# RMSNorm on one core: every second group's sums of squares go through PSUM, squared four rows at a time on ScalarE and summed on VectorE

## The chip, the cores and the metric

The kernel runs on one core of a Trainium2 chip. The metric is the device time of one execution in microseconds (us). For the kernel before it is 163.68 us, the median of 10 runs that lie between 163.41 and 164.09.

## The reference

```python
def reference(x, gamma):              # x: 16 x 1024 x 512 f32, gamma: 512
    eps = 1e-5
    rms = np.sqrt(np.mean(x ** 2, axis=-1, keepdims=True) + eps)
    return (x / rms * gamma).astype(np.float32)
```

There are 16,384 rows of 512 values. Each row is divided by the root of the mean of its squares and multiplied by gamma. The kernel reads 33.55 MB and writes as much.

## The kernel before

The rows are cut into four blocks of 4,096 rows (8.39 MB each). In a block each of the 128 partitions holds 32 rows of 512 values. SBUF has three buffers of that size, `slot0` to `slot2`; blocks 0, 1 and 2 each get one, and block 3 is loaded into `slot0` once block 0 has been stored from there.

**Transfers.** All large transfers are issued by SyncE (SP), in one queue, in the order of the program: block 0 in two halves of 16 rows (called load 0a and load 0b here), block 1, block 2; then store 0 (whole), store 1a (rows 0 to 15), load 3a, load 3b, store 1b, store 2 (whole), store 3a, store 3b. SP waits at each one until what it needs is there: a store for the multiplies of its rows, load 3a and load 3b for the landing of store 0 (they overwrite its buffer). What stands behind a waiting transfer is not issued until the wait is over. Half a block is 4.19 MB.

**Computation.** `compute(slot, r0, r1)` walks over groups of `G = 8` rows. There are 16 groups in all, numbered 0 to 15 here: 0 to 3 are block 0, 4 to 7 block 1, and so on; store 0 needs groups 0 to 3, store 1a groups 4 and 5, store 1b groups 6 and 7, store 2 groups 8 to 11, store 3a groups 12 and 13, store 3b groups 14 and 15. For each group:

- ScalarE squares each row by itself (line 70) and accumulates the sum of the squares into one column of `ss`; on the engine this is an ACTIVATE and a short ACTIVATION_READ_ACCUMULATOR. The squares themselves go to `sq_scratch` and are not read.
- ScalarE takes the root of `ss / 512 + eps` into `rms` (line 76). The first root is preceded by a table load.
- VectorE takes the reciprocal into `rstd` (line 77) and multiplies each row, in place, by its `rstd` and by gamma (line 79, one SCALAR_TENSOR_TENSOR for each row).

Each engine works through its own queue in order. Before the loop gamma is spread over the 128 partitions by a matmul with a column of ones (line 56) and copied from PSUM to SBUF by VectorE (line 58). The order on ScalarE and VectorE before is that of the program: eight squares and a root for each group on ScalarE, a reciprocal and eight multiplies for each group on VectorE.

Of the kernel before, what the change touches and what calls it, by code (L numbers as in the profile page):

```python
# [1 line left out]

# [4 lines left out]


@with_exitstack
def kernel(  # L10
    ctx: ExitStack,
    tc: tile.TileContext,
    x: bass.AP,
    gamma: bass.AP,
    out: bass.AP,
):
    nc = tc.nc
    P = nc.NUM_PARTITIONS
    eps = 1e-5
    fp32 = mybir.dt.float32  # L20
    AF = mybir.ActivationFunctionType
    OP = mybir.AluOpType

    xf = x.flatten_outer_dims()
    of = out.flatten_outer_dims()
    N, D = xf.shape
    R = 32
    G = 8
    assert N == 4 * P * R

    xv = xf.rearrange("(t p r) d -> t p r d", p=P, r=R)
    ov = of.rearrange("(t p r) d -> t p r d", p=P, r=R)

    const = ctx.enter_context(tc.tile_pool(name="const", bufs=1))
    stats = ctx.enter_context(tc.tile_pool(name="stats", bufs=4))
    psum = ctx.enter_context(tc.tile_pool(name="psum", bufs=1, space=bass.MemoryType.PSUM))

    slots = [const.tile([P, R, D], fp32, name=f"slot{i}") for i in range(3)]

    def load(t, slot, r0, r1):  # L40
        nc.sync.dma_start(out=slots[slot][:, r0:r1], in_=xv[t][:, r0:r1])

    def store(t, slot, r0, r1):
        nc.sync.dma_start(out=ov[t][:, r0:r1], in_=slots[slot][:, r0:r1])

    load(0, 0, 0, 16)
    load(0, 0, 16, 32)
    load(1, 1, 0, 32)
    load(2, 2, 0, 32)

    gamma_row = const.tile([1, D], fp32)
    nc.scalar.dma_start(out=gamma_row, in_=gamma.unsqueeze(0))
    ones_col = const.tile([1, P], fp32)
    nc.vector.memset(ones_col, 1.0)  # L54
    gamma_psum = psum.tile([P, D], fp32)
    nc.tensor.matmul(gamma_psum, ones_col, gamma_row, start=True, stop=True)  # L56
    gamma_b = const.tile([P, D], fp32)
    nc.vector.tensor_copy(out=gamma_b, in_=gamma_psum)  # L58

    eps_t = const.tile([P, 1], fp32)  # L60
    nc.vector.memset(eps_t, eps)  # L61
    sq_scratch = const.tile([P, D], fp32)

    def compute(slot, r0, r1):
        for g in range(r0, r1, G):
            ss = stats.tile([P, G], fp32, name="ss")
            rms = stats.tile([P, G], fp32, name="rms")
            rstd = stats.tile([P, G], fp32, name="rstd")
            for r in range(G):
                nc.scalar.activation(  # L70
                    out=sq_scratch,
                    in_=slots[slot][:, g + r, :],
                    func=AF.Square,
                    accum_out=ss[:, r : r + 1],
                )
            nc.scalar.activation(out=rms, in_=ss, func=AF.Sqrt, bias=eps_t, scale=1.0 / D)  # L76
            nc.vector.reciprocal(out=rstd, in_=rms)  # L77
            for r in range(G):
                nc.vector.scalar_tensor_tensor(  # L79
                    out=slots[slot][:, g + r, :],  # L80
                    in0=slots[slot][:, g + r, :],
                    scalar=rstd[:, r : r + 1],
                    in1=gamma_b,
                    op0=OP.mult,
                    op1=OP.mult,
                )

    compute(0, 0, 32)
    store(0, 0, 0, 32)
    compute(1, 0, 16)  # L90
    store(1, 1, 0, 16)
    load(3, 0, 0, 16)
    load(3, 0, 16, 32)
    compute(1, 16, 32)
    store(1, 1, 16, 32)
    compute(2, 0, 32)
    store(2, 2, 0, 32)
    compute(0, 0, 16)
    store(3, 0, 0, 16)
    compute(0, 16, 32)  # L100
    store(3, 0, 16, 32)


# [1 line left out]
_INS = ['x', 'gamma']  # L105
_OUTS = [((16, 1024, 512), 'float32')]


# [23 lines left out]
```

## Time and profile before

| | before |
|---|---|
| median of 10 runs | 163.68 us |
| the profiled execution | 163.41 us |
| its span | 161.6 us |
| VectorE idle before the first reciprocal, until a root came | 15.27 us, ended at 20.41 us |
| HBM read and written | 33.56 MB and 33.55 MB, 415 GB/s over the span |

The span is the part of the execution that the trace covers, from its first to its last record; 1.8 us of the execution lie outside it. All points in time count from the start of the span. In the page, L70 is line 70, ACT is ScalarE and DVE is VectorE, and a row of the list of groups gives operation, output and input, shapes, number, then busy time in all and the mean of one in ns, then the idle time of the engine just before these instructions. The DMA row of the picture in slices has a digit for each fortieth of the span, the busy share of the 16 DMA engines in tenths.

### The profile page before, as it was taken

Reading aid. Unit: us, or ns where it says so; the run is one execution under the profiler, and the core shown is the slowest. Engines: PE = TensorE matmul, PEld = TensorE weight load, DVE = VectorE, ACT = ScalarE, POOL = GpSimd, SP = SyncE. Lnnn points to the kernel's source line nnn. Section 1 sums busy time; section 2 is a strip of 40 time slices with the busy share of each in tenths; the row PEclk is TensorE's granted clock in tenths of the full one; section 3 lists DMA queues with packets and bytes.
Section 4 is the critical chain, followed back from the end, with each engine's and each line's share of the span. In section 5 each row is a group of like instructions: output and inputs, shape, how many; then the busy total and the mean of one; then the engine's idle time right before and its main releaser. Section 6 shows DMA issues by size and latency. Waiting matters only on the chain.

```text
span 161.6 us, 509 instructions
## 1 busy us (share of the span) xinstructions
PE 2.0 (1%) x2; PEld 0.5 (0%) x2; DVE 90.3 (56%) x147; ACT 98.5 (61%) x274; POOL 0.2 (0%) x4
## 2 busy tenths in 40 slices
PE   4000000000000000000000000000000000000000
PEld 1000000000000000000000000000000000000000
DVE  0100098988909898898898892019889890000000
ACT  3008999996599999999999700699999400000000
POOL 0000000000000000000000000000000000000000
DMA  7999999998998999699699999999999799799990
GB/s 260 389 414 495 389 438 470 519 391 389 519 405 373 505 276 487 292 503 503 292 481 414 397 487 414 397 487 414 397 511 503 341 454 503 308 462 414 422 462 41
DMA packets 1733, 67.14 MB, mean 415 GB/s; under 512 B 193, under 2 KB 193, under 8 KB 194
## 3 DMA queue, kind: packets, MB, share of 16 engines
q1 hardware_dynamic: 1728, 67.11, 97.2%
q14 instruction: 3, 0.02, 0.0%
q10 hardware_dynamic: 2, 0.00, 0.0%
HBM read 33.56 MB, written 33.55 MB: 415 GB/s over the span
## 4 chain that ended last, share of the span: by engine, by line
DMA 43%; ACT 20%; DVE 17%; issue 2%; DVEq 0%
DMA out_dram<-slot 24%; DMA slot<-in_x_dram 19%; ACT sq_scratch L70 18%; DVE slot L79 16%; ACT rms L76 2%; ACT L76 1%; DVE rstd L77 1%; DVEq L127 0%
## 5 line engine op out<-in xcount | busy, mean ns | idle before, releaser
L70 ACT ACTIVATE sq_scratch<-slot 128x512 f32<-128x512 f32 x128 | 80.5, 629 | 27.0 <-DMA slot<-in_x_dram 23.5
L79 DVE SCALAR_TENSOR_TENSOR slot<-slot,rstd,gamma_b 128x512 f32<-128x512 f32 x128 | 86.2, 747 | 0.6
L77 DVE RECIPROCAL rstd<-rms 128x8 f32<-128x8 f32 x16 | 3.2, 203 | 37.8 <-ACT rms L76 37.8
L70 ACT ACTIVATION_READ_ACCUMULATOR sq_scratch<-slot 128x1 f32 x128 | 23.9, 187 | 0.0
L76 ACT ACTIVATE rms<-ss,eps_t 128x8 f32<-128x8 f32 x16 | 4.8, 301 | 0.5
L58 DVE COPY gamma_b<-gamma_psum 128x512 f32<-128x512 f32 x1 | 0.7, 692 | 3.5 <-PE gamma_psum L56 3.5
L56 PE MATMUL gamma_psum<-gamma_row,ones_col 1*128 1x512 f32 x2 | 2.0, 1122 | 2.4 <-DMA gamma_row<-in_gamma_dram 2.4
L70 ACT ACT_TABLE_LOAD x1 | 1.3, 1283 | 1.3 <-PEq L116 1.3
L76 ACT ACT_TABLE_LOAD x1 | 1.3, 1283 | 0.0
L54 DVE MEMSET ones_col<- 1x128 f32 x1 | 0.2, 165 | 0.8 <-PEq L116 0.8
L56 PEld LDWEIGHTS gamma_psum<-gamma_row,ones_col 1*128 1x128 f32 x2 | 0.5, 306 | 2.3 <-issue 2.3
L116 POOL MEMSET const-bfloat16-1.0<- 128x1 bf16 x1 | 0.1, 101 | 0.0
L116 POOL MEMSET const-uint8-127<- 128x1 uint8 x1 | 0.1, 101 | 0.0
L116 POOL MEMSET const-float32-0.0<- 128x1 f32 x1 | 0.1, 98 | 0.2 <-issue 0.2
L116 POOL MEMSET const-float32-1.0<- 128x1 f32 x1 | 0.1, 98 | 0.0
L61 DVE MEMSET eps_t<- 128x1 f32 x1 | 0.1, 59 | 0.0
## 6 DMA issues: line engine op xcount, KB each, us to landing
slot<-in_x_dram SPq DMA_DIRECT2D x4, 4096.0 KB, 19.4
out_dram<-slot SPq DMA_DIRECT2D x4, 4096.0 KB, 31.2
slot<-in_x_dram SPq DMA_DIRECT2D x2, 51.0
out_dram<-slot SPq DMA_DIRECT2D x2, 40.7
gamma_row<-in_gamma_dram ACTq DMA_DIRECT2D x1, 2.0 KB
```

The source lines that it names most:

```text
L54: nc.vector.memset(ones_col, 1.0)
L56: nc.tensor.matmul(gamma_psum, ones_col, gamma_row, start=True, stop=True)
L58: nc.vector.tensor_copy(out=gamma_b, in_=gamma_psum)
L61: nc.vector.memset(eps_t, eps)
L70: nc.scalar.activation(out=sq_scratch, in_=slots[slot][:, g + r, :], func=AF.Square, accum_out=ss[:, r : r + 1],)
L76: nc.scalar.activation(out=rms, in_=ss, func=AF.Sqrt, bias=eps_t, scale=1.0 / D)
L77: nc.vector.reciprocal(out=rstd, in_=rms)
L79: nc.vector.scalar_tensor_tensor(out=slots[slot][:, g + r, :], in0=slots[slot][:, g + r, :], scalar=rstd[:, r : r + 1], in1=gamma_b, op0=O ...
L116: nc = _bacc.Bacc("TRN2", target_bir_lowering=False, num_devices=1)
```

## The change

In the groups with an odd number the eight accumulating squares are replaced. ScalarE squares four rows with one instruction (128 partitions x 2,048 values) into a PSUM tile `sq`, and VectorE sums each of the four rows in it with one `tensor_reduce`, into four columns of `ss`. Two such pairs make a group. `sq` takes 8 KB of each partition, and the pool has two of them. The tile in which gamma is spread now comes from the same pool. The even groups stay as they were.

```diff
+    H = 4
-    psum = ctx.enter_context(tc.tile_pool(name="psum", bufs=1, space=bass.MemoryType.PSUM))
+    psum = ctx.enter_context(tc.tile_pool(name="psum", bufs=2, space=bass.MemoryType.PSUM))
...
-    gamma_psum = psum.tile([P, D], fp32)
-    nc.tensor.matmul(gamma_psum, ones_col, gamma_row, start=True, stop=True)
+    gamma_psum = psum.tile([P, H, D], fp32, name="sq")
+    nc.tensor.matmul(gamma_psum[:, 0], ones_col, gamma_row, start=True, stop=True)
     gamma_b = const.tile([P, D], fp32)
-    nc.vector.tensor_copy(out=gamma_b, in_=gamma_psum)
+    nc.vector.tensor_copy(out=gamma_b, in_=gamma_psum[:, 0])
...
-            for r in range(G):
-                nc.scalar.activation(
-                    out=sq_scratch,
-                    in_=slots[slot][:, g + r, :],
-                    func=AF.Square,
-                    accum_out=ss[:, r : r + 1],
-                )
+            if (g // G) % 2:
+                for h in range(0, G, H):
+                    sq = psum.tile([P, H, D], fp32, name="sq")
+                    nc.scalar.activation(out=sq, in_=slots[slot][:, g + h : g + h + H, :], func=AF.Square)
+                    nc.vector.tensor_reduce(
+                        out=ss[:, h : h + H], in_=sq, axis=mybir.AxisListType.X, op=OP.add
+                    )
+            else:
+                for r in range(G):
+                    nc.scalar.activation(
+                        out=sq_scratch,
+                        in_=slots[slot][:, g + r, :],
+                        func=AF.Square,
+                        accum_out=ss[:, r : r + 1],
+                    )
             nc.scalar.activation(out=rms, in_=ss, func=AF.Sqrt, bias=eps_t, scale=1.0 / D)
```

The layer under the kernel orders the instructions of an engine by itself, and with this change it interleaves groups. The two queues of the changed program are, with q4 x1 for one accumulating square of a row of group 4, S5a and S5b for the two four-row squares of group 5, R5a and R5b for their sums, rt4 for the root, rc4 for the reciprocal and m4 for the eight multiplies of group 4:

```
ScalarE
q0 x1, S1a, q0 x1, S1b, q0 x6, table load, rt0, rt1
q2 x1, S3a, q2 x1, S3b, q2 x6, rt2, rt3
q4 x1, S5a, q4 x1, S5b, q4 x1, S7a, q4 x1, S7b, q4 x4, rt4, rt5
q6 x8, rt6
q8 x1, S9a, q8 x7, q10 x1, rt7, rt8
S9b, q10 x1, S11a, q10 x6, rt9, rt10, S11b, rt11
q12 x1, S13a, q12 x1, S13b, q12 x6, rt12, rt13
q14 x1, S15a, q14 x1, S15b, q14 x6, rt14, rt15

VectorE
R1a, R1b, rc0, rc1, m0, m1
R3a, rc2, R3b, m2, rc3, m3
R5a, R5b, rc4, R7a, m4, rc5, rc6, m5, m6
R7b, R9a, rc7, rc8, m7, m8
R9b, R11a, rc9, rc10, m9, m10, R11b, rc11, m11
R13a, R13b, rc12, rc13, m12, m13
R15a, rc14, R15b, m14, rc15, m15
```

The order of the transfers on SP is unchanged.

## The prediction

> **What bounds the kernel now.** First the page's slices and DMA queues, to see whether a resource is full.
>
> ```profile
> PE 2.0 (1%) x2; PEld 0.5 (0%) x2; DVE 90.3 (56%) x147; ACT 98.5 (61%) x274; POOL 0.2 (0%) x4
> DMA  7999999998998999699699999999999799799990
> q1 hardware_dynamic: 1728, 67.11, 97.2%
> ```
>
> SP's queue keeps the 16 DMA engines busy for 97.2% of the span; no compute engine passes 61%. The kernel is bound by its transfers, and computation matters only where it hands over a store after the queue has run empty. So next: how late may each store come? The chain of waits, the timeline of VectorE's last group and the DMA answer for the last store:
>
> ```profile
> 0.72 12.02 DMA slot<-in_x_dram
> ...
> 44.75 38.12 DMA out_dram<-slot
> ```
> ```profile
> 127.33 0.20 DVE L77 RECIPROCAL rstd<-rms 128x8 f32<-128x8 f32 x1 [0.61 <-ACT rms L76]
> 127.57 5.39 DVE L79 SCALAR_TENSOR_TENSOR slot<-slot,rstd,gamma_b 128x512 f32<-128x512 f32 x8
> ```
> ```profile
> out_dram<-slot SPq DMA_DIRECT2D x1, 4096.0 KB, 27.6
> ```
>
> A half block into an empty queue lands 12.02 us after its issue. The last store is issued at 133.0, when the multiplies end, and lands 27.6 us later, at 160.6: over half of that is queueing. The DMA records (packets of the queue, split by their 4-byte markers) show the transfers strictly in turn, 9.68 us for each half block. Counting back 1.0 us from issue to first packet, no DMA engine idles if store 0 is issued by 60.5, store 1a by 79.8, store 1b by 108.9, store 2 by 118.5, store 3a by 137.9 and store 3b by 147.5. Before, they come at 44.8, 60.6, 83.8, 98, 120.5 and 133.0: 14.5 to 25 us early. **That margin of 14.5 us at the last store is what the change may spend.** It can gain next to nothing, since earlier stores would only queue.
>
> **The prices.** The list of groups:
>
> ```profile
> L70 ACT ACTIVATE sq_scratch<-slot 128x512 f32<-128x512 f32 x128 | 80.5, 629 | 27.0 <-DMA slot<-in_x_dram 23.5
> L79 DVE SCALAR_TENSOR_TENSOR slot<-slot,rstd,gamma_b 128x512 f32<-128x512 f32 x128 | 86.2, 747 | 0.6
> L77 DVE RECIPROCAL rstd<-rms 128x8 f32<-128x8 f32 x16 | 3.2, 203 | 37.8 <-ACT rms L76 37.8
> L70 ACT ACTIVATION_READ_ACCUMULATOR sq_scratch<-slot 128x1 f32 x128 | 23.9, 187 | 0.0
> L76 ACT ACTIVATE rms<-ss,eps_t 128x8 f32<-128x8 f32 x16 | 4.8, 301 | 0.5
> L58 DVE COPY gamma_b<-gamma_psum 128x512 f32<-128x512 f32 x1 | 0.7, 692 | 3.5 <-PE gamma_psum L56 3.5
> ```
>
> Instructions overlap, so I use steps, not means. Multiplies: eight take 5.39 = 7 steps + 0.747, a step of 0.665 and a tail of 0.08. Accumulating square with its read: 0.752 (pairs in the chain start that far apart). Root 0.31, table load 1.3, reciprocal up to the next multiply 0.24.
>
> - **Removed from ScalarE:** 64 accumulating squares, 64 x 0.752 = 48.1 us.
> - **Added to ScalarE:** 16 four-row squares, 128x2048. Not in the trace. From below: the squares against the root, (629 - 301) / 504 = 0.65 ns a value, give 0.629 + 1536 x 0.65 ns = 1.63. From above: four separate ones, 2.52. [...]
> - **Added to VectorE:** 16 sums of 128x2048 from PSUM. Not in the trace. From above: four times the nearest row, the copy of 512 from PSUM, less overlap: 4 x 0.692 - 0.08 = 2.69. [...] Multiply against reciprocal, (747 - 203) / 504 = 1.08 ns a value, gives 0.692 + 1.66 - 0.08 = 2.27. I take **2.25**. Sum 36.0; VectorE goes from 90 to 126 us busy.
>
> [...]
>
> **The walk through the queues.** The built order decides how much of the 36 us is hidden.
>
> 1. ScalarE starts at 12.76, when load 0a lands. Ahead of root 0 it now has 8 x 0.752 + 2 x 1.83 + 1.3 + 0.31 = 11.3. The first reciprocal starts at 24.08 (before 20.41); sums R1a and R1b lie in that wait, free.
> 2. From there VectorE has 128 x 0.665 = 85.1, 16 x 0.24 = 3.8 and 14 x 2.25 = 31.5, together 120.4, and is nearly always the later engine.
> 3. One real hole. ScalarE's S7a and S7b stand ahead of root 4 and need PSUM tiles that R5a and R5b free; these stand behind group 3's multiplies, which end at 51.0. R5a ends at 53.2, R5b at 55.4; from 53.2 ScalarE needs 2 x 1.83 + 5 x 0.752 + 0.31 = 7.7 to finish root 4 at 61.0. **VectorE idles 5.6 us.** ScalarE's own waits there (5.0 for a tile) cost nothing further.
> 4. Small holes: R11b, root 11, reciprocal 11 in turn, 0.44; others 0.3. Root 11 holds back all of block 3 on ScalarE (until 113.9), but its transfers landed by 112.3 and groups 12 and 13 are ready before VectorE is.
>
> Sum: 24.1 + 120.4 + 5.6 + 0.8 + 0.1 = **151.0**, the issue of store 3b, 18 us later than before. The same walk gives 51.0 for store 0, 74.7, 90.3, 119.5 and 135.3 for the others: only store 2 (by 1 us) and store 3b (by 3.5) come after the queue may idle, and store 3b alone sets the end. The waits that SP gains on ScalarE for load 3a and 3b are for squares long done.
>
> The end: 151.0 + 11.8 = 162.8, against 160.6. I take 11.8 rather than 12.02, because the first packets of load 0a took 1.5 to 2.1 us where later ones take 1.21. The loss is less than 3.5 because an empty queue lets the lagging DMA engine catch up: the last store's parts landed over 2.0 us before. So 163.41 + 2.2 = **165.6 us**. The profiled execution was among the shortest of the ten; I add nothing for the median (0.27 higher), since the new path never waits for a transfer after 12.76.
>
> Zero lies at an issue by 160.6 - 11.8 = 148.8. From the walk, 0.1 us on a sum moves the end by 1.3, on a four-row square by 0.4.
>
> **The rivals.**
>
> - **The margin holds (not slower), 16%.** Mechanism: VectorE's sum is cheap enough. Place: the 13 sums on its path; point: below 2.08 us each, or other steps 2.2 us shorter in all, the last store is issued by 148.8. For it: the margin is large and my overlap guesses are coarse. [...] Half of this I count as within 0.2%, half as faster.
> - **The sum pays per row, 8%.** If each 512-value row costs like the copy, 2.69: issue 156.8, end 168.6, time 171.4. [...]
> - **VectorE late by the forecast, 76%.** Sums 2.13 to 2.4 and squares 1.63 to 1.95 give 163.9 to 168.4.
>
> That the change doesn't act is out: the built queues hold the 16 squares and 16 sums.
>
> Range 163.4 to 168.8, leaving out the per-row case and about half of the first. A measurement of this kernel tells 0.2% (0.33 us) from no change. Slower 0.83, same 0.08, faster 0.09.
>
> **What would show it.** VectorE near 126 us busy, with the new row of sums at 2.3 us mean (tail included) and four-row squares at 1.9; the first reciprocal at 24.1; a VectorE hole of 5 to 6 us before reciprocal 4, around 55 to 61; last multiplies ending at 151; the last store landing 11.5 to 12 us after its issue instead of 27.6; the DMA share dipping just before 152. A last store that still queues for well over 12 us would mean that the margin held; sums far from 2.3 us would break the sum.

## The result and the profile after

The changed kernel takes 162.63 us, the median of 14 runs (162.28 to 163.32). The kernel before takes 163.59 us, the median of 51 runs with those on the same chips (162.72 to 164.50). The ratio is 0.9942, interval 0.9928 to 0.9955: **faster by 0.6%**, where 165.6 us and slower had been forecast. The profiled execution took 162.42 us, its span is 160.6 us.

These are the lines of the page after: engine totals, DMA picture, the two DMA queues, and the rows of the groups that changed.

```profile
span 160.6 us, 402 instructions
...
PE 2.0 (1%) x2; PEld 0.5 (0%) x2; DVE 123.4 (77%) x163; ACT 79.9 (50%) x162; POOL 0.2 (0%) x4
...
DMA  7999999969969999898999999999996996999993
...
q1 hardware_dynamic: 1728, 67.11, 97.8%
q14 instruction: 2, 0.02, 0.0%
...
L88 DVE SCALAR_TENSOR_TENSOR slot<-slot,rstd,gamma_b 128x512 f32<-128x512 f32 x128 | 85.7, 747 | 0.1
L79 ACT ACTIVATE sq_scratch<-slot 128x512 f32<-128x512 f32 x64 | 40.0, 625 | 13.8 <-DMA slot<-in_x_dram 12.5
L74 DVE TENSOR_REDUCE ss<-sq 128x4 f32<-128x2048 f32 x16 | 36.1, 2277 | 10.5 <-ACT sq L73 10.4
L73 ACT ACTIVATE sq<-slot 128x2048 f32<-128x2048 f32 x16 | 29.7, 1859 | 4.8 <-DVE ss L74 4.8
```

VectorE did take on the forecast load (123.4 us), ScalarE did become lighter (98.5 to 79.9 us), and the transfers stay the full resource (97.8%). The same two queue lines before show what the forecast passed over:

```profile
span 161.6 us, 509 instructions
...
q1 hardware_dynamic: 1728, 67.11, 97.2%
q14 instruction: 3, 0.02, 0.0%
```

Queue 14, of the kind "instruction" in the page, fetches the program's own instructions, 8,192 bytes each time in the DMA records, on the same 16 DMA engines: at each fetch of the two executions one of the engines leaves a gap of 0.30 us between two packets of data. Before there are three such fetches in the span, after there are two. In the DMA records they start at 33.9, 53.3 and 83.0 us before, at 45.9 and 64.2 after.

The stores, from VectorE's timeline after (start, duration, instruction, idle time before it): its hole in the middle, and its end.

```profile
49.90 4.48 DVE L74 TENSOR_REDUCE ss<-sq 128x4 f32<-128x2048 f32 x2
59.77 0.20 DVE L86 RECIPROCAL rstd<-rms 128x8 f32<-128x8 f32 x1 [5.39 <-ACT rms L85]
...
142.17 0.20 DVE L86 RECIPROCAL rstd<-rms 128x8 f32<-128x8 f32 x1
142.40 5.39 DVE L88 SCALAR_TENSOR_TENSOR slot<-slot,rstd,gamma_b 128x512 f32<-128x512 f32 x8
```

The hole before reciprocal 4 is there. The last multiplies end at 147.8, not at 151.0. The view of that last store alone, after:

```profile
L45 SPq DMA_DIRECT2D out_dram<-slot x1: 332/332/332, 147.8 to 147.8; - x1
...
DMA to landing us min/median/max: 11.8/11.8/11.8
```

It lands at 147.8 + 11.8 = 159.6, 1 us ahead of the 160.6 before, although it was issued 14.8 us later.

**Where the microsecond came from.** The DMA records hold a 4-byte marker for each DMA engine at the end of each transfer (192 in each execution, for 12 transfers), so they show how far the 16 engines are apart. The engine that finishes first is nearly the same in the two executions: its store 3a ends at 148.5 before and 148.4 after. The last one differs. Spread between first and last engine, in us, at the end of six of the transfers:

| | load 0b | block 1 | block 2 | store 1a | load 3b | store 3a |
|---|---|---|---|---|---|---|
| before | 0.54 | 0.96 | 1.70 | 1.70 | 2.05 | 2.05 |
| after | 0.36 | 0.36 | 0.94 | 1.08 | 1.19 | 1.19 |

Every transfer here is cut into equal shares for the 16 engines (1,728 packets, 108 for each engine over the whole kernel), so one that has fallen behind stays behind (1.70 us before from block 2 to store 1a, 2.05 from load 3b to store 3a), and the last landing is that of the slowest. The 1.0 us between the two landings is this spread (2.05 - 1.19 = 0.86) and the 0.13 of the fastest engine. The packets of one engine follow each other within a few ns, so they can be strung together engine by engine. An engine that took a fetch started its next packet 0.30 us late, and that packet took longer as well: 2.73, 3.02 and 1.33 us at the three fetches before, where 2.42, 2.42 and 1.21 are usual in this trace. So a fetch put its engine back by 0.6, 0.9 and 0.4 us.

Before, the fetches at 33.9 and 83.0 fell on one DMA engine, which ended 1.53 behind the first. The fetch at 53.3 fell on another, which lost 0.45 more in a stretch near 58 in which all engines were slow, and 0.35 in a single packet at 109. That one is the last, 2.05 behind. So in this one execution the fetch that is missing after the change, the one at 83.0, did not set the end; what its absence is worth has to come from the runs below. In "after" the slowest engine never ran dry: 149.6 + 9.68 = 159.3, its marker of the last store. So a late store that lets lagging engines catch up can't have made the gain here.

### The profile page after: what moved, and what is told of

Read it like the earlier page. It is cut to its first block, busy times and chain, and to the rows that moved or that the text cites. A ratio compares the mean times of both kernels' runs of the same rounds, so it can differ in the third digit from the quotient of the medians.

```text
span 160.6 us, 402 instructions
## 1 busy us (share of the span) xinstructions
PE 2.0 (1%) x2; PEld 0.5 (0%) x2; DVE 123.4 (77%) x163; ACT 79.9 (50%) x162; POOL 0.2 (0%) x4
## 3 DMA queue, kind: packets, MB, share of 16 engines
q1 hardware_dynamic: 1728, 67.11, 97.8%
## 4 chain that ended last, share of the span: by engine, by line
DVE 71%; ACT 12%; DMA 7%; issue 1%; DVEq 0%
DVE slot L88 52%; DVE ss L74 18%; DMA slot<-in_x_dram 7%; ACT sq_scratch L79 6%; ACT sq L73 4%; DVE rstd L86 1%; ACT L85 1%; ACT rms L85 1%; DVEq L136 0%
## 5 line engine op out<-in xcount | busy, mean ns | idle before, releaser
L79 ACT ACTIVATE sq_scratch<-slot 128x512 f32<-128x512 f32 x64 | 40.0, 625 | 13.8 <-DMA slot<-in_x_dram 12.5
L74 DVE TENSOR_REDUCE ss<-sq 128x4 f32<-128x2048 f32 x16 | 36.1, 2277 | 10.5 <-ACT sq L73 10.4
L73 ACT ACTIVATE sq<-slot 128x2048 f32<-128x2048 f32 x16 | 29.7, 1859 | 4.8 <-DVE ss L74 4.8
L79 ACT ACTIVATION_READ_ACCUMULATOR sq_scratch<-slot 128x1 f32 x64 | 11.9, 186 | 0.0
L59 DVE COPY gamma_b<-sq 128x512 f32<-128x512 f32 x1 | 0.7, 692 | 3.2 <-PE sq L57 3.2
L57 PE MATMUL sq<-gamma_row,ones_col 1*128 1x512 f32 x2 | 2.0, 1122 | 2.1 <-DMA gamma_row<-in_gamma_dram 2.1
L57 PEld LDWEIGHTS sq<-gamma_row,ones_col 1*128 1x128 f32 x2 | 0.5, 308 | 2.1 <-issue 2.1
```

The lines of the kernel that those rows point to most:

```text
L57: nc.tensor.matmul(gamma_psum[:, 0], ones_col, gamma_row, start=True, stop=True)
L59: nc.vector.tensor_copy(out=gamma_b, in_=gamma_psum[:, 0])
L73: nc.scalar.activation(out=sq, in_=slots[slot][:, g + h : g + h + H, :], func=AF.Square)
L74: nc.vector.tensor_reduce(out=ss[:, h : h + H], in_=sq, axis=mybir.AxisListType.X, op=OP.add)
L79: nc.scalar.activation(out=sq_scratch, in_=slots[slot][:, g + r, :], func=AF.Square, accum_out=ss[:, r : r + 1],)
```

## The experiments

Theory F says that fewer instructions on ScalarE mean fewer fetches, and that the lag which fetches cause in single DMA engines sets the end. Rivals: D, the late last store empties the queue and lets laggards catch up; T, VectorE's walk still ends the kernel; C, the gain comes from other order or lighter traffic, or the lags are chance. Eleven kernels were run, all in several rounds against the kernel before on the same chips. Fetches and spread are those of each run's profiled execution; the spread is that at the end of store 3a, as above.

| run | median us | ratio to before (interval) | fetches | spread |
|---|---|---|---|---|
| short_sum | 162.58 | 0.9938 (0.9917 to 0.9958) | 2 | 1.33 |
| transfers | 162.15 | 0.9902 (0.9877 to 0.9928) | 0 | 1.07 |
| transfers_fill | 164.99 | 1.0073 (1.0044 to 1.0102) | 4 | 3.56 |
| after_fill | 164.86 | 1.0064 (1.0044 to 1.0084) | 6 | 3.59 |
| act_fill | 163.10 | 0.9979 (0.9964 to 0.9994) | 3 | 1.55 |
| no_sums | 162.59 | 0.9950 (0.9935 to 0.9965) | 2 | 0.96 |
| late | 165.04 | 1.0099 (1.0067 to 1.0131) | 2 | 1.62 |
| before_shift | 163.41 | 0.9995 (0.9976 to 1.0014) | 3 | 2.16 |
| after_fill1 | 163.76 | 1.0015 (1.0000 to 1.0030) | 4 | 2.56 |
| no_sums_fill | 163.23 | 1.0001 (0.9977 to 1.0026) | 3 | 2.01 |
| scratch_psum | 163.39 | 1.0005 (0.9987 to 1.0023) | 3 | 1.50 |

That the spread sets the end holds throughout: the time of the profiled execution less its spread is between 161.2 and 161.6 us in all of them, the kernels before and after included, except in late (163.4), whose queue ran dry. But the spread of one execution has chance in it: late is the changed kernel up to its last group and has 1.62 where the change has 1.19. What an edit costs is therefore read from the medians.

**short_sum**, on the changed kernel:

```diff
-                        out=ss[:, h : h + H], in_=sq, axis=mybir.AxisListType.X, op=OP.add
+                        out=ss[:, h : h + H], in_=sq[:, :, 0:128], axis=mybir.AxisListType.X, op=OP.add
```

> The changed kernel, but each sum reads only the first 128 of the 512 squares of a row, so that sums over a quarter of the values are computed in the odd groups. Same number of instructions on each engine as the change, VectorE some 20 us earlier at the end. Theory F (fewer instructions on ScalarE mean fewer instruction fetches, each of which holds one DMA engine up; the lag of that engine sets the end): still 2 fetches, the time stays at 162.2 to 162.8, although the last store is issued near 127 and queues for over 30 us. Rival D (the late last store finds the queue running dry, which lets lagging DMA engines catch up): with the store early again the gain goes, 163.3 to 163.8. Rival T (VectorE's walk is still what ends the kernel): 161.5 or less.

162.58 us. The last store alone:

```profile
L45 SPq DMA_DIRECT2D out_dram<-slot x1: 332/332/332, 134.9 to 134.9; - x1
...
DMA to landing us min/median/max: 25.2/25.2/25.2
```

It is issued at 135, some 13 us earlier than in the change (less than the 20 expected) and queues again, and the time is that of the change. D and T fall: neither a late last store nor VectorE's end decides in the changed kernel.

**transfers**, on the kernel before:

```diff
-    compute(0, 0, 32)
     store(0, 0, 0, 32)
-    compute(1, 0, 16)
     store(1, 1, 0, 16)
...
```

> Only the transfers: the normalization is left out and the output is the input; the twelve transfers and the preparation of gamma stay, in the same order on SP. The floor of the transfers. Theory F: no instruction fetch in the span, the DMA engines end within 0.7 us of each other, time 161.3 to 162.2, below the change. Rival D: no store comes late, lags add up as before, 163.2 to 163.8. Rival C (lags are chance and contention on memory, whatever the instructions): between, 162.3 to 163.3.

162.15 us, without a fetch in the span. This is the floor of these twelve transfers: the kernel before stands 1.6 us above it in the same rounds (163.75), the change about 0.5. The spread of the profiled execution, one of its longer ones, was somewhat wider than the 0.7 expected; half of it came near 109, in one step and without any fetch.

**transfers_fill** (on transfers) and **after_fill** (on the change), the same edit:

```diff
+    fill = const.tile([P, 1], fp32)
+    for i in range(512):
+        nc.gpsimd.memset(fill, float(i))
     gamma_row = const.tile([1, D], fp32)
```

> The transfers alone as in the run beside it, with 512 memsets of 128x1 on GpSimd, which nothing waits for. Theory F: some four instruction fetches of 8 KB appear in the span, each holds one DMA engine up by 0.4 to 0.9 us, on one engine where it is the same program's queue; the last landing comes 0.7 to 3 us later than in the run without them. Rivals C and D: no change within 0.3 us.

> The changed kernel with 512 memsets of 128x1 on GpSimd, which nothing waits for; VectorE and ScalarE as in the change. Theory F: four more fetches, 163.3 to 165.3. Rivals C and D: 162.3 to 163.0 as the change.

164.99 us against 162.15, and 164.86 against 162.63: 2.2 to 2.8 us for memsets that nobody waits for. The queue lines of transfers_fill:

```profile
q1 hardware_dynamic: 1728, 67.11, 96.3%
q14 instruction: 4, 0.03, 0.0%
```

They share no data with the transfers. The DMA records of transfers_fill show how they act: 15 engines stay within 0.71 us of each other to the end, and one falls behind, 0.82 by load 0b, 1.49 after the fetch at 32.2, 3.09 by the end of block 2, 3.49 after the fetch at 71.8. All four fetches (11.0, 32.2, 52.2, 71.8) struck the same engine, and its share of the last store is what the kernel waits for. Not all of its lag is the fetches themselves: of the 1.60 gained in block 2, the fetch at 52.2 is 0.66, and the rest was lost in the slow stretch that follows, near 58 to 61. Rivals C and D fall for these runs.

**act_fill**, on the change: give ScalarE back enough instructions for a second fetch.

```diff
+    fill = const.tile([P, 1], fp32)
+    for i in range(40):
+        nc.scalar.activation(out=fill, in_=eps_t, func=AF.Square)
+
     def compute(slot, r0, r1):
```

> The changed kernel with 40 squares of 128x1 put ahead of the first square on ScalarE, in the time in which it waits for load 0a; VectorE's queue and the stores as in the change. It gives ScalarE over 200 instructions again, enough to reach a second instruction fetch (before fetched for ScalarE near its 60th and 191st instruction). Theory F: 3 fetches in the span, two of them holding up the same DMA engine; the last landing 0.4 to 0.9 us later than with the change, time 162.9 to 163.6. Rival C (the gain came from the lighter traffic of ScalarE, or from the order of the groups): no change, 162.3 to 162.8.

163.10 us: half of the gain is gone. The page has the third fetch, and in the DMA records it comes at 120.8, when ScalarE has started 184 instructions. ScalarE's two fetches are at 17.0 and 120.8, not at 33.9 and 83.0; both fall on one DMA engine, and it is the last one (1.55). The other half of the gain is not explained by this run.

```profile
q1 hardware_dynamic: 1728, 67.11, 97.5%
q14 instruction: 3, 0.02, 0.0%
```

**no_sums**, on the change: the ScalarE half alone.

```diff
                     nc.scalar.activation(out=sq, in_=slots[slot][:, g + h : g + h + H, :], func=AF.Square)
-                    nc.vector.tensor_reduce(
-                        out=ss[:, h : h + H], in_=sq, axis=mybir.AxisListType.X, op=OP.add
-                    )
+                ss = ones_ss
```

> The ScalarE half of the change alone: four-row squares in the odd groups, but VectorE doesn't sum them; the root of these groups is taken of a constant. The sums of squares of the odd groups are left out. Last store issued some 30 us before the change's. Theory F: 2 fetches, 162.2 to 162.8, as the change. Rival D (a late last store gives the gain): 163.3 or more. If VectorE's later end costs the change anything: up to 0.2 us below it.

162.59 us. The whole gain is in the ScalarE half; the 36 us of sums on VectorE cost nothing that can be measured.

**late**, on the change, tests how the prediction turned a late store into time.

```diff
-    compute(0, 16, 32)
+    compute(0, 16, 24)
+    late = const.tile([P, 1], fp32)
+    nc.vector.tensor_reduce(
+        out=late, in_=slots[0][:, 16:22].rearrange("p r d -> p (r d)"), axis=mybir.AxisListType.X, op=OP.add
+    )
+    compute(0, 24, 32)
```

> The changed kernel with one more VectorE instruction (a sum over six rows, 3.3 us, read by nobody) ahead of the last group's reciprocal, so that the last store is issued near 151, where the prediction had put it. The prediction's conversion (issue + 11.8 us to the landing): landing near 162.9, time 165.4 to 165.9, every DMA engine dry before. If the queue still held work beyond the lag seen so far: below 164.5.

165.04 us, between the two expectations. The last store alone:

```profile
L45 SPq DMA_DIRECT2D out_dram<-slot x1: 332/332/332, 151.1 to 151.1; - x1
...
DMA to landing us min/median/max: 11.1/11.1/11.1
```

The store into the empty queue took 11.1 us here, not 11.8. All engines ended within 0.16 us, so the queue did run dry and the laggards did catch up; still the kernel is 2.4 us slower than the change. Past the edge the mechanism of the forecast is real.

**before_shift** (on the kernel before) and **after_fill1** (on the change) were meant to refine the theory, and neither went as set up.

```diff
+    fill = const.tile([P, 1], fp32)
+    for i in range(15):                  # before_shift; 192 in after_fill1
+        nc.vector.memset(fill, float(i)) # before_shift; nc.gpsimd in after_fill1
```

> The kernel before with 15 memsets of 128x1 on VectorE ahead of its work, in the time in which it waits for load 0a. The number of fetches stays 3, but VectorE's fetch, which came near its 52nd instruction at 53 us, amid the load of block 2, moves some 10 us earlier. If theory F's count alone matters (ScalarE's second fetch): no change, 163.3 to 163.8. If where VectorE's fetch falls matters as well (it was followed by the largest lag of the trace, 1.7 us): 162.8 to 163.2.

163.41 us, no change, but the fetch did not move either: 53.2 against 53.3. So this run says nothing on where a fetch hurts most, and it leaves open whose fetch this is. In before_shift and the kernel before VectorE has started 67 and 52 instructions by then, ScalarE 105 in each.

> The changed kernel with 192 memsets of 128x1 on GpSimd, enough for one fetch of GpSimd's. If the fetches of each compute engine go to a DMA engine of their own and the worst lag decides, not the sum: a third fetch, but at most 0.3 us more than the change, 162.5 to 162.9. If every fetch adds to the end: 163.1 to 163.6.

163.76 us. The 192 memsets brought two fetches of GpSimd's (11.1 and 32.2), not one. The slowest engine ends 2.56 behind the first, the next one 0.79. With 0, 2 and 4 fetches for GpSimd the change takes 162.63, 163.76 and 164.86: 0.5 to 0.6 us for each, what such an engine loses in the slow stretch near 58 included. The expectation that they would hide behind the others' lag does not hold for two. Whether one would hide is open.

**no_sums_fill** (on no_sums) and **scratch_psum** (on the kernel before) go for the other half of the gain.

```diff
                 ss = ones_ss
+                for i in range(14):
+                    nc.scalar.activation(out=fill, in_=slots[slot][:, g + 4, i : i + 1], func=AF.Square)
```

> The kernel with four-row squares and without the sums of the odd groups (left out, as in no_sums), with 14 squares of 128x1 added to each odd group on ScalarE, so that ScalarE has about as many instructions as before, spread over the span as before; stores early. Theory F (the number of ScalarE's instructions, through its fetches, is the whole gain): 3 fetches, 163.3 to 163.8, as before the change. If only part of the gain is ScalarE's second fetch and the rest lighter traffic or other order: 162.9 to 163.2.

163.23 us beside 163.29 for the kernel before in the same batch, ratio 1.0001. With ScalarE's instruction count restored (287 records of it against 294 before; no_sums has 175), spread over the span, the gain of no_sums is gone, though its squares and its order of groups stay. Engine totals and queue lines of this run:

```profile
PE 2.0 (1%) x2; PEld 0.5 (0%) x2; DVE 89.1 (55%) x148; ACT 91.6 (57%) x274; POOL 0.2 (0%) x4
...
q1 hardware_dynamic: 1728, 67.11, 97.3%
q14 instruction: 3, 0.02, 0.0%
```

ScalarE's fetches stand at 34.0 and 82.0 here, within 1 us of those before, and 60 and 190 instructions had started by then, against 60 and 191. The fetch between them is at 61.9, as in no_sums (61.8), so its place is not what took the gain away. Both of ScalarE's fetches fall on one DMA engine, and that engine ends last (2.01); it is so in before_shift (2.16) and scratch_psum (1.50) too. In no_sums ScalarE has one fetch, at 46.0. How much of the gain is the second fetch that is missing, and how much the later place of the first, these runs do not separate.

```diff
-    sq_scratch = const.tile([P, D], fp32)
+    sq_scratch = psum.tile([P, D], fp32, name="sq_scratch")
```

> The kernel before, with the unread squares written to a PSUM tile in place of the SBUF one: the same instructions and order, less writing into SBUF by ScalarE. Theory F: 3 fetches, no change, 163.3 to 163.8. If ScalarE's writes into SBUF slow the transfers: 162.7 to 163.2.

163.39 us, no change. The last form of rival C, ScalarE's writes into SBUF, falls.

The experiments point to still fewer instructions, down to the floor of 162.15. No such version was run: ScalarE's first fetch came when it had started 60 instructions before and 51 in the change (at 33.9 and 45.9 us), and a further cut moves sums to VectorE, which by an estimate has only some 1 to 2 us left before its last store is late (issued at 147.8, against 160.6 - 11.1 = 149.5).

## Why the prediction was wrong

Point by point, by its own steps.

- **"It can gain next to nothing, since earlier stores would only queue": this failed, and it turned the sign.** The floor was taken from the trace before as if the transfers owned their engines. Some 1.6 us of that time stood above the floor that transfers shows, as lag between the DMA engines, part of it caused by the program's own instruction fetches (0.6, 0.9 and 0.4 us on the engines that took the three). ScalarE went from 294 recorded instructions to 169, and its fetch near the 190th did not happen. no_sums_fill gives it back and the gain is gone (163.23 us). The 2.0 us between the engines at the end was seen and used, as lag that an empty queue would absorb, but its origin was not asked for. The line that told it, the count on queue 14, stood directly under the quoted one.
- **The issue of store 3b, 151.0: mis-sized.** It measured 147.8. Some 0.4 us came ahead of the first reciprocal (23.70, not 24.08). The reciprocals took 2.4 in all, not 3.8: 0.24 held only where the multiply waited for that very reciprocal (0.23 at 142.17), and with a sum or a second reciprocal between them they cost some 0.1 (0.11 at 36.9). The 14 sums took steps of 2.19, not 2.25 (0.8 in all), the multiplies 0.662, not 0.665 (0.3), and the hole 5.39, not 5.6. All errors had one sign, and 2.2 us was all that separated the forecast from its first rival. With the issue at 147.8 the 2.2 us of forecast loss fell away whole; the other 0.8 us of the miss is the lag above (from the profiled 163.41 to 162.63). The bounds given for the main case were mis-summed as well: by the forecast's own 1.3 and 0.4 for each 0.1 us they are 163.2 to 168.0, not 163.9 to 168.4. Its low end is an issue at 148.6, already the rival's ground.
- **The first rival's point, an issue by 148.8: right in kind.** late makes it 160.6 - 11.1 = 149.5 with the measured time into an empty queue. The change came in at 147.8, so the margin held, as short_sum and no_sums confirm. The rival was given 16%; its reason, a cheap sum below 2.08 us, was not what happened: the sum's mean was 2.277, its step 2.19.
- **What was right:** VectorE's 126 us (123.4), the means of the new rows (2.28 and 1.86 for 2.3 and 1.9), the 5.6 us hole and its place, and what is taken off ScalarE (98.5 to 79.9, 18.6 us, where the steps used, 64 x 0.752 - 16 x 1.83, give 18.8). With the forecast's own issue time, as in late, the kernel takes 165.0, near the 165.6 forecast.
- **Right by luck:** the 11.8 us to the landing. It was forecast for an empty queue, into which the store of late took 11.1. In the change the slowest engine was still at store 3a for 1.8 us when the last store was issued, then needed its 9.68, and 0.3 to the landing. So this sign could not tell a late store from one in time. The dip of the DMA share before 152 did not come: the slices there read 9.
- **Two prices without a run:** no run shows the 1.83 us that the walk takes for a four-row square and that stands in its 24.1 and 5.6, nor the 2.13 us at the low end for a sum. In the change a four-row square has a mean of 1.859 us, and the next instruction on ScalarE starts 1.80 after its start (13.38 to 15.18 us); the 24.1 and 5.6 came out as 23.70 and 5.39; the sums take 2.24 to 2.29 us, with a step of 2.19. The 2.27 worked out from the rows before stands beside a mean of 2.277.
- **ScalarE's load:** at 61% busy its time was not what limited the kernel. Fewer and larger operations on it paid all the same (no_sums 162.59), but through the fetches and not through ScalarE's time (no_sums_fill 163.23).

## What to carry to other kernels

Where the page shows the DMA engines full (97.2% here), compare the engines' ends, and ask what each laggard was given besides its share: here the last landing was that of the slowest engine, 2.05 us behind the first before and 1.19 after at the end of store 3a. Look at the count on the instruction queue as well: 512 unrolled memsets on the otherwise idle GpSimd brought four fetches here, and cost 2.2 to 2.8 us that no engine's row shows. Where a forecast rests on a margin of 1 to 2%, a sum of a hundred steps needs each step as it stands next to its neighbours, not one price for all.

## What was not expected of the hardware

- A fetch of 8,192 bytes occupied its DMA engine for 0.31 us in the records, but the engine fell further behind, by 0.4 to 0.9 us (0.42 at 83.0 before, 0.67 at 32.2 in transfers_fill, 0.9 at 53.3 before). GpSimd's four fetches all fell on one engine in transfers_fill, and ScalarE's two on one engine before, so they added up. On ScalarE the two fetches of the kernel before are 131 started instructions apart.
- Near 58 us, in the load of block 2, all engines have a packet that takes about 1.3 us longer (3.2 to 4.2 us where 2.42 is usual), before and after alike, and without a fetch in the transfers alone too. An engine that was already behind lost more there, 0.9 us in transfers_fill. What it is stays open, as does which DMA engine a fetch falls on and whose fetch the one at 53 us was.
